# Attention tiles ordered long and short in turn, and the low part of k multiplied by the high part of q alone, the two maps in the two halves of the array's rows

## The chip, the cores and the metric

The kernel runs on one core of one Trainium2 chip. The metric is the device time of one execution in microseconds (us). Before the change the median of 3 runs is 2411.27 us (2409.47 to 2414.34).

## What is computed

The reference is one inference step of a two-layer encoder for a prompt (1 x 1024 tokens) and a sample group (8 streams x 16 tokens with 256 cached keys each), model width 1024, 8 heads. The part that the change touches is the differential attention: two softmax maps per head over 64-wide halves of q and k, chunk-causal for the prompt, unmasked over cache and new tokens for the sample.

```
def diff_attend(q, k, v, lam, mask):
    s = jnp.einsum('bqhmd,bkhmd->bhmqk', q, k).astype(jnp.float32) * (HEAD_DIM ** -0.5)
    if mask is not None:
        s = jnp.where(mask, s, -jnp.inf)
    p = jax.nn.softmax(s, axis=-1)
    a = p[:, :, 0] - lam * p[:, :, 1]
    return jnp.einsum('bhqk,bkhv->bqhv', a.astype(v.dtype), v)
```

Around it, each layer has an input projection, a pooling branch, gates (silu and sigmoid of projections), output projections and a LayerNorm.

## The kernel before, in words

Each layer runs in stages: projections of v, q and k, the pooling branch, then the attention stage (556 to 1010 us and 1750 to 2203 us of the profile), then the merge and the output projection. Large products are made in fp32r, with both operands split into a high and a low part: high x high, low x high, high x low.

The attention stage has two streams that one loop braids (lines 1384 to 1405). The filler (`filler`, line 968) computes gates for what follows: 16 weight tiles x 3 column groups x 8 steps, 384 steps of three matmuls with 384 columns (`tmm_steps`, lines 320 to 322), each chunk of 8 steps followed by a tanh on ScalarE (line 977) and, for 8 of the 16 weight tiles, a multiplication on VectorE (line 980). The attention (`attention`, line 1280) is a generator that yields a number after each piece of work; the loop multiplies it by `share` (line 1388) and runs so many filler steps. The numbers stand in `STEPS` (line 48): 54 a head.

A head has nine items: eight query tiles of 128 rows, 0 to 7, where tile i has 128 x (i + 1) keys, and the decode item "d" for all eight streams. An item's work is:

- `s1`: scores on TensorE into PSUM. A tile up to 3 uses one two-bank score buffer for both maps (lines 1062 to 1068), a longer tile one buffer for each map (lines 1079 to 1088); there are two buffers (`ps_two`). The operand `qs` holds q's high part in rows 0 to 63 and its low part in rows 64 to 127, and `kh` and `kl` hold k's high and low part twice, so one 128-row matmul gives (high + low of q) x (a part of k).
- `soft`: mask and negated maximum on VectorE (lines 1071 and 1072, or 1093 and 1094), exponentials with row sums on ScalarE (1076, 1096).
- `mix`: VectorE makes one map of two (1105 to 1109).
- `s2a`: transposes of the mixed map on TensorE (1119), copies by ScalarE to the tile `at` (1121). For "d" VectorE reduces the transposes into `azt` and `atl` (1196, 1198).
- `s2b`: the product with v on TensorE (1144; for "d" 1207 and 1214, on 32 columns of the array each), a copy to `osb` on VectorE (1126) and, later, squares on ScalarE.

An engine takes its instructions in the order in which this code issues them. In a slot (one item of the loop from line 1299 on) the order is: `s1` of item n, `s2a` of item n-2 (from slot 6 on, n-1), `soft` of n, first filler part, `s2b` of the same older item, `mix` of n, other work of the head, second filler part. The items come as "d", 0, 1, ... 7 (0, 1, "d", 2 to 7 in head 0), the last tile's second half in the next head's first slot.

For the next head, `prep_load` fetches q and k, `prep_split` splits them (ScalarE copies, lines 902 and 903, VectorE subtractions, 904 and 905), `load_dec`, `load_v` and `load_vc` fetch the decode keys and the values. All transfers are issued on SyncE's queue, in order. After a head, `post_a`, `post_f` and `post_b` normalise and transpose its output.

Of the kernel before, what the change touches and what calls it, by code (L numbers as in the profile page):

```python
# [17 lines left out]
P = 128  # L18
# [8 lines left out]
NG = 3  # L27
# [20 lines left out]
STEPS = [(3, 2), (2, 2), (4, 1), (2, 2), (2, 2), (3, 3, 4), (3, 4), (3, 4), (4, 4)]  # L48
MG = 4
HIP = False  # L50
HEAD0 = 8
YG = 2
# [11 lines left out]
def trunk(ctx, tc, a):  # L64
# [393 lines left out]
    for l in range(DEPTH):  # L458
# [435 lines left out]
        def prep_split(h, m):  # L894
# [6 lines left out]
            qs, kh, kl = mk("qs"), mk("kh"), mk("kl")  # L901
            S.copy(qs, sq)
            S.copy(kh, sk)
            V.tensor_tensor(out=qs[64:, :], in0=sq[64:, :], in1=qs[64:, :].bitcast(F32), op=ALU.subtract)
            V.tensor_tensor(out=kl, in0=sk, in1=kh.bitcast(F32), op=ALU.subtract)
            heads[h][m] = (qs, kh, kl)
# [47 lines left out]
        for tag, shape, bufs in (("osb", [P, 9, P], 2), ("gsb", [P, GW], 2), ("th", [P, GW], 3), ("atl", [P, P], 1),  # L954
                                 ("at", [P, 512], 2)):
            ap.tile(shape, F32, tag=tag, name=tag, bufs=bufs)
        for name in ("qs0", "kh0", "kl0"):
            ap.tile([P, SEQ], F32R, tag=name, name=name)
        ap.tile([P, 1024], F32, tag="p", name="p", bufs=3)
# [48 lines left out]
        ITEMS = ["d", 0, 1, 2, 3, 4, 5, 6, 7]  # L1008
# [45 lines left out]
        def s1_tile(h, i):  # L1054
# [7 lines left out]
            if n <= 512:  # L1062
                cw = max(n, 256)
                s = ps_two()
                for m in range(2):
                    qs, kh, kl = hd[m]
                    PE.matmul(s[:, m, :cw], qs[:, ql], kh[:, :cw], start=True, stop=False)
                    PE.matmul(s[:, m, :cw], qs[:, ql], kl[:, :cw], start=False, stop=True)
# [11 lines left out]
            sps = []  # L1080
            for m in range(2):
                qs, kh, kl = hd[m]
                s = ps_two()
                for b in range(2):
                    kc = slice(b * c, b * c + c)
                    PE.matmul(s[:, b, :c], qs[:, ql], kh[:, kc], start=True, stop=False)  # L1086
                    PE.matmul(s[:, b, :c], qs[:, ql], kl[:, kc], start=False, stop=True)  # L1087
                sps.append(s)
# [191 lines left out]
        def attention():  # L1280
# [9 lines left out]
            load_dec(0)  # L1290
# [4 lines left out]
            for h in range(H):  # L1295
                start_head(h)
                nxt = h + 1 < H
                items = ITEMS if h else [0, 1, "d"] + ITEMS[3:]
                for n, i in enumerate(items):
                    f1, f2 = STEPS[n][:2]  # L1300
                    soft = s1_dec(h) if i == "d" else s1_tile(h, i)
                    if n == 0:
# [423 lines left out]
```

## Time and profile before

| | |
|---|---|
| runs | 2411.27 us median (2409.47 to 2414.34, n = 3) |
| the profiled execution | 2411.42 us, its span 2409.6 us |
| granted TensorE clock, mean | 0.993 |
| busy share of the span | PE 96%, weight loads 90%, DVE 64%, ACT 41%, POOL 12% |
| DMA | 379.09 MB, 157 GB/s |
| attention stages | 556 to 1010 us, 1750 to 2203 us |

PE is TensorE's matmuls and PEld its weight loads, which overlap them; DVE is VectorE, ACT ScalarE, POOL GpSimd, SPq the queue of transfers. Lines such as L1144 are lines of the kernel. A timeline row gives the start in us, the duration, engine, line, operation, out<-in, shapes, count, and in brackets the idle time before it and what ended it. A row of waits gives the waiting instruction, what released it, and microseconds in total, the number of times, and where a third number stands the longest. A row of groups gives the count, then busy time in us and mean ns of one, then the idle time before. The duration of a matmul includes its way through the array; neighbours overlap, so the time that one occupies is read from the starts of two neighbours.

### The profile page before, as it was taken

How to read it: one execution, taken by the hardware profiler on the slowest of the kernel's cores; microseconds unless marked ns; L12 is line 12 of the kernel's file. 1: busy time of each engine (PE TensorE's matmuls, PEld its weight loads, DVE VectorE, ACT ScalarE, POOL GpSimd, SP SyncE). 2: the span in 40 equal slices, each digit the busy share in tenths (PEclk: the TensorE clock that was granted, in tenths of full speed). 3: DMA queues.
4: the chain of work that ended last, by engine and by line, in shares of the span. 5: the costliest groups of instructions: out<-in, count | busy, mean ns of one | idle time of the engine just before them, and what ended most of it. 6: DMA issues, size and time to landing. Idle time of an engine off the chain costs nothing.

```text
span 2409.6 us, 39819 instructions
## 1 busy us (share of the span) xinstructions
PE 2304.1 (96%) x14928; PEld 2157.8 (90%) x14928; DVE 1546.1 (64%) x2980; ACT 977.8 (41%) x2177; POOL 296.6 (12%) x312
## 2 busy tenths in 40 slices
PE   7999999998999999999999999999989999999998
PEld 6889999998888888898878999999988888889986
DVE  4477855546777777756524787546367777775855
ACT  8432234213555555523533232342145555554122
POOL 1023310000000000032100233000000000001433
PEclk9999999999999999999999999999999999999999
DMA  6643344656544554486336433445664555446942
GB/s 214 219 116 102 103 104 108 200 174 203 150 139 140 151 165 128 152 288 249 122 118 202 115 101 99 116 116 175 201 180 140 146 161 161 145 120 207 316 166 78
DMA packets 247714, 379.09 MB, mean 157 GB/s; under 512 B 49889, under 2 KB 190177, under 8 KB 247521
## 3 DMA queue, kind: packets, MB, share of 16 engines
q1 hardware_dynamic: 247520, 376.55, 50.9%
q8 instruction: 117, 1.92, 0.3%
q14 instruction: 77, 0.62, 0.1%
HBM read 259.67 MB, written 117.83 MB: 157 GB/s over the span
## 4 chain that ended last, share of the span: by engine, by line
PE 70%; DVE 11%; DMA 7%; ACT 6%; issue 4%; SPq 1%; POOL 1%; ACTq 0%; DVEq 0%; POOLq 0%
PE ps_lin L598 5%; PE ps_lin L596 5%; PE ps_lin L597 5%; PE ps_lin L320 5%; PE ps_lin L321 5%; PE ps_lin L322 5%; PE ps_tr L1144 4%; PE ps_tr L596 2%; PE ps_tr L598 2%; PE ps_tr L597 2%; PE ps_lin L335 2%; PE ps_lin L336 2%; PE ps_lin L334 2%; ACT p L1076 2%; PE ps_tr L1119 2%
## 5 line engine op out<-in xcount | busy, mean ns | idle before, releaser
L320 PE MATMUL ps_lin<-xh,wh 128*128 128x384 f32 x952 | 345.3, 363 | 1.1 <-ACT xh L1267 0.7
L322 PE MATMUL ps_lin<-xh,wl 128*128 128x384 f32 x952 | 321.3, 337 | 0.0
L321 PE MATMUL ps_lin<-xl,wh 128*128 128x384 f32 x952 | 320.7, 337 | 0.3 <-DVE xl L1270 0.2
L320 PEld LDWEIGHTS ps_lin<-xh,wh 128*128 128x128 f32 x952 | 180.4, 189 | 5.6 <-issue 2.8
L1144 PE MATMUL ps_tr<-vt,at 128*128 128x128 f32 x1152 | 156.2, 282 | 28.1 <-ACT at L1121 28.1
L1144 PEld LDWEIGHTS ps_tr<-vt,at 128*128 128x128 f32 x1152 | 147.2, 195 | 39.2 <-ACT at L1121 38.6
L321 PEld LDWEIGHTS ps_lin<-xl,wh 128*128 128x128 f32 x952 | 180.8, 190 | 1.1 <-DVE xl L1270 0.8
L322 PEld LDWEIGHTS ps_lin<-xh,wl 128*128 128x128 f32 x952 | 179.5, 189 | 0.0
L1121 ACT COPY at<-ps_tr 128x512 f32<-128x512 f32 (+1 forms) x192 | 85.8, 482 | 172.1 <-PE ps_tr L1119 172.1
L1096 ACT ACTIVATE p<-ps_two,anm 128x640 f32<-128x640 f32 (+3 forms) x128 | 122.3, 962 | 33.4 <-DVE anm L1094 29.8
L1076 ACT ACTIVATE p<-ps_two,anm 128x128 f32<-128x128 f32 (+3 forms) x128 | 66.4, 524 | 168.6 <-DVE anm L1072 160.3
L1094 DVE TENSOR_REDUCE anm<-ps_two 128x1 f32<-128x640 f32 (+3 forms) x128 | 131.2, 1025 | 4.4
L270 DVE TENSOR_TENSOR wl<-ws,wh 128x1024 fp32r<-128x1024 f32 (+1 forms) x74 | 86.0, 1162 | 70.8 <-ACT wh L265 67.6
L265 ACT CAST wh<-ws 128x1024 fp32r<-128x1024 f32 (+1 forms) x74 | 74.1, 1002 | 115.4 <-PE ps_lin L321 49.7
L640 POOL TENSOR_TENSOR tt<-tt 128x288 f32<-128x288 f32 x64 | 63.1, 986 | 420.4 <-DVE tt L639 257.2
L1108 DVE SCALAR_TENSOR_TENSOR p<-p,acc 128x128 f32<-128x128 f32 (+7 forms) x128 | 104.8, 818 | 4.5
L1086 PE MATMUL ps_two<-kh,qs 128*128 128x320 f32 (+3 forms) x256 | 91.0, 357 | 11.3 <-ACT p L1076 11.3
L1119 PE MATMUL ps_tr<-ident,p 128*128 128x128 f32 x576 | 84.4, 273 | 5.6 <-DVE r L1109 5.6
L1087 PE MATMUL ps_two<-kl,qs 128*128 128x320 f32 (+3 forms) x256 | 89.5, 352 | 0.0
L1126 DVE COPY osb<-ps_tr 128x128 f32<-128x128 f32 x144 | 41.3, 287 | 66.1 <-PE ps_tr L1144 60.4
L659 ACT COPY sb<-ps_lin 128x288 f32<-128x288 f32 x80 | 32.0, 400 | 123.3 <-PE ps_lin L598 118.8
L1119 PEld LDWEIGHTS ps_tr<-ident,p 128*128 128x128 f32 x576 | 69.2, 141 | 13.0 <-ACT xh L1267 6.2
(522 smaller groups left out, 6886.9 us busy)
## 6 DMA issues: line engine op xcount, KB each, us to landing
ws<-wt SPq DMA_DIRECT2D x96, 512.0 KB, 4.0
mt_d<-th SPq DMA_DIRECT2D x96, 192.0 KB, 3.2
fx<-q_d SPq DMA_DIRECT2D x128, 128.0 KB, 3.4
fx<-o_k SPq DMA_DIRECT2D x128, 128.0 KB, 3.3
st<-ck SPq DMA_DIRECT2D x32, 512.0 KB, 5.9
fx<-cv SPq DMA_DIRECT2D x32, 512.0 KB, 4.0
mt<-mt_d SPq DMA_DIRECT2D x42, 384.0 KB, 5.8
xT_d<-xs SPq DMA_DIRECT2D x36, 256.0 KB, 2.6
```

The lines of the kernel that those rows point to most:

```text
L320: PE.matmul(ps, wh[:, k, :], xh[:, k, :], start=(k == 0), stop=False),
L321: PE.matmul(ps, wh[:, k, :], xl[:, k, :], start=False, stop=False),
L322: PE.matmul(ps, wl[:, k, :], xh[:, k, :], start=False, stop=(k == nk - 1)))
L596: PE.matmul(ps, wh[:, k, :], oh[:, k, :], start=first and k == 0, stop=False, **more)
L597: PE.matmul(ps, wh[:, k, :], ol[:, k, :], start=False, stop=False, **more)
L598: PE.matmul(ps, wl[:, k, :], oh[:, k, :], start=False, stop=k == 3, **more)
L1076: S.activation(out=pt[m], in_=s[:, m, :n], func=AF.Exp, bias=nm[:, m:m + 1], accum_out=ls_[:, m:m + 1])
L1094: V.tensor_reduce(out=nm[:, m:m + 1], in_=s[:, :, :c], axis=AX.XY, op=ALU.max, negate=True)
L1096: S.activation(out=p[:, :n].rearrange("p (b c) -> p b c", b=2), in_=s[:, :, :c], func=AF.Exp, bias=nm[:, m:m + 1], accum_out=ls_[:, m:m + 1])
L1108: V.scalar_tensor_tensor(out=pt[0], in0=pt[1], scalar=cc, in1=pt[0], op0=ALU.mult, op1=ALU.add)
L1119: PE.transpose(tr[:, j * P:(j + 1) * P], p[:, (b0 + j) * P:(b0 + j + 1) * P], ident)
L1144: PE.matmul(o_ps, hd["at", i][b // 4][:, (b % 4) * P:(b % 4 + 1) * P], hd["vt", b // 4][:, b % 4, :], start=(b == 0), stop=(b == i))
```

## The change

Four things change, all in the attention stage.

**Items.** They come as 7, 3, 6, 2, 5, 1, 4, 0, "d" (in the last head 7, 3, 6, 2, 5, "d", 4, 1, 0), in one flow of 72 slots over all heads, with two more slots at the end. In slot j: `s1` of item j, `s2a` of item j-2, `soft` of j, `mix` of j-1, squares, first filler part, `s2b` of j-2, other work, second filler part. The loads, splits and post-processing move to other slots: the split of the next head's second map to the start of slot 8, the decode keys to slot 2 of their own head, the decode values to slot 8 (in the last head slot 3).

**Filler.** `STEPS` has 52 steps a head, and `share` is computed for 28 steps fewer (`REST`), so that 365 of the 384 steps fall into the attention generator and the others run after it.

**Low part of k.** The product of q's low part with k's low part is left out. The low parts of k of both maps share one tile `kl`: map 0 in rows 0 to 63, map 1 in rows 64 to 127. For map 1, `qs` has its high part in rows 64 to 127. The high matmuls of both maps come first, on 128 rows; then the low matmuls on 64 rows each, map 0 in the upper half of the array's rows and map 1 in the lower half, in turn.

**Small.** The tiles that were allocated ahead at the start of the stage no longer are, and what the last heads' output waits for before its split is 5 rounds in place of 2 (line 1382).

```diff
-STEPS = [(3, 2), (2, 2), (4, 1), (2, 2), (2, 2), (3, 3, 4), (3, 4), (3, 4), (4, 4)]
+STEPS = [(2, 3), (5, 1), (3, 2), (3, 4), (3, 2), (3, 4), (3, 2), (3, 3), (3, 3)]
+REST = 28
...
-            qs, kh, kl = mk("qs"), mk("kh"), mk("kl")
+            qs, kh = mk("qs"), mk("kh")
+            if m == 0:
+                heads[h]["kl"] = mk("kl")
+            kl = heads[h]["kl"]
+            hi, lo = (slice(m * 64, m * 64 + 64), slice(64 - m * 64, 128 - m * 64))
             S.copy(qs, sq)
             S.copy(kh, sk)
-            V.tensor_tensor(out=qs[64:, :], in0=sq[64:, :], in1=qs[64:, :].bitcast(F32), op=ALU.subtract)
-            V.tensor_tensor(out=kl, in0=sk, in1=kh.bitcast(F32), op=ALU.subtract)
-            heads[h][m] = (qs, kh, kl)
+            V.tensor_tensor(out=qs[lo, :], in0=sq[lo, :], in1=qs[lo, :].bitcast(F32), op=ALU.subtract)
+            V.tensor_tensor(out=kl[hi, :], in0=sk[hi, :], in1=kh[hi, :].bitcast(F32), op=ALU.subtract)
+            heads[h][m] = (qs, kh, kl[hi, :], hi)
...
-        ITEMS = ["d", 0, 1, 2, 3, 4, 5, 6, 7]
+        ITEMS = [7, 3, 6, 2, 5, 1, 4, 0, "d"]
+        LAST = [7, 3, 6, 2, 5, "d", 4, 1, 0]
...
                 for m in range(2):
-                    qs, kh, kl = hd[m]
+                    qs, kh, _, _ = hd[m]
                     PE.matmul(s[:, m, :cw], qs[:, ql], kh[:, :cw], start=True, stop=False)
-                    PE.matmul(s[:, m, :cw], qs[:, ql], kl[:, :cw], start=False, stop=True)
+                for m in range(2):
+                    qs, _, kl, hi = hd[m]
+                    PE.matmul(s[:, m, :cw], qs[hi, ql], kl[:, :cw], start=False, stop=True)
...
-            sps = []
+            sps = [ps_two() for _ in range(2)]
             for m in range(2):
-                qs, kh, kl = hd[m]
-                s = ps_two()
                 for b in range(2):
-                    kc = slice(b * c, b * c + c)
-                    PE.matmul(s[:, b, :c], qs[:, ql], kh[:, kc], start=True, stop=False)
-                    PE.matmul(s[:, b, :c], qs[:, ql], kl[:, kc], start=False, stop=True)
-                sps.append(s)
+                    PE.matmul(sps[m][:, b, :c], hd[m][0][:, ql], hd[m][1][:, b * c:b * c + c], start=True, stop=False)
+            for b in range(2):
+                for m in range(2):
+                    qs, _, kl, hi = hd[m]
+                    PE.matmul(sps[m][:, b, :c], qs[hi, ql], kl[:, b * c:b * c + c], start=False, stop=True)
...
+            flow = [(h, n, i) for h in range(H) for n, i in enumerate(ITEMS if h < H - 1 else LAST)]
+            for j in range(len(flow) + 2):
+                h, n, i = flow[j] if j < len(flow) else (H, j - len(flow), None)
+                back = flow[j - 2] if j >= 2 else None
+                last = h == H - 1
+                f1, f2 = STEPS[n]
+                if n == 0 and h < H:
+                    start_head(h)
+                if n == 8 and not last:
+                    if h + 1 < H:
+                        prep_split(h + 1, 1)
+                soft = None
+                if i is not None:
                     soft = s1_dec(h) if i == "d" else s1_tile(h, i)
+                if back:
+                    s2a(back[0], back[2])
+                if soft:
                     soft()
+                if 0 < j <= len(flow):
+                    mix(flow[j - 1][0], flow[j - 1][2])
+                do_squares()
+                yield f1
+                if back:
+                    s2b(back[0], back[2])
...
+                yield f2
...
-                ylive.append([h, g, 2])
+                ylive.append([h, g, 5])
...
-        share = len(gate_order) * NG * KD / (H * sum(map(sum, STEPS)) + HEAD0)
+        share = (len(gate_order) * NG * KD - REST) / (H * sum(map(sum, STEPS)) + HEAD0)
```

What stands on TensorE for tile 5 of the second head before: the eight score matmuls, map 0 in buffer `ps_two_6730` and map 1 in `ps_two_6735`, each high matmul followed by its low one, and the transposes of tile 4.

```order
L1086 MATMUL ps_two_6730<-kh_6047,qs_6046 128x384
L1087 MATMUL ps_two_6730<-kl_6048,qs_6046 128x384
L1086 MATMUL ps_two_6730<-kh_6047,qs_6046 128x384
L1087 MATMUL ps_two_6730<-kl_6048,qs_6046 128x384
L1086 MATMUL ps_two_6735<-kh_6283,qs_6282 128x384
L1087 MATMUL ps_two_6735<-kl_6284,qs_6282 128x384
L1086 MATMUL ps_two_6735<-kh_6283,qs_6282 128x384
L1087 MATMUL ps_two_6735<-kl_6284,qs_6282 128x384
L1119 MATMUL ps_tr_6740<-ident_72,p_6635 128x128 x4
```

The same place on TensorE now, for tile 6 of the first head, with the transposes of tile 7 behind it (L1085 and L1089 are the high and the low matmul, L1120 the transposes).

```order
L1085 MATMUL ps_two_5757<-kh_5524,qs_5523 128x448 x2
L1085 MATMUL ps_two_5758<-kh_5657,qs_5656 128x448 x2
L1089 MATMUL ps_two_5757<-kl_5525,qs_5523 128x448
L1089 MATMUL ps_two_5758<-kl_5525,qs_5656 128x448
L1089 MATMUL ps_two_5757<-kl_5525,qs_5523 128x448
L1089 MATMUL ps_two_5758<-kl_5525,qs_5656 128x448
L1120 MATMUL ps_tr_5767<-ident_72,p_5699 128x128 x4
```

The low matmuls have moved behind all the high ones and alternate between the two maps, and both read one tile `kl_5525`; both buffers are complete only with the last two rows.

On VectorE, the decode item and tile 0 of the second head before: maximum of "d" (L1166), its mixing (L1179 to L1182), then maximum of tile 0 (L1072) and its mixing (L1105 to L1109).

```order
L1166 TENSOR_REDUCE dnm_6337<-ps_two_6311 128x2
L980 SCALAR_TENSOR_TENSOR th_6351<-th_6351,ps_lin_6257 128x384
L1126 COPY osb_5703<-ps_tr_6356 128x128
L1179 RECIPROCAL drc_6366<-dls_6339 128x2
L1180 TENSOR_SCALAR drc_6366<-drc_6366,sgn_4682 128x2
L1182 TENSOR_SCALAR p_6340<-p_6340,drc_6366 128x384 x2
L1071 MEMSET ps_two_6381 64x2x64
L1072 TENSOR_REDUCE anm_6380<-ps_two_6381 128x2
L1105 RECIPROCAL ar2_6399<-als_6379 128x1
L1107 SCALAR_TENSOR_TENSOR acc_6401<-als_6379,nlam_4681,ar2_6399 128x1
L1108 SCALAR_TENSOR_TENSOR p_6388<-p_6388,acc_6401 128x128
```

And on VectorE now, tiles 4 and 1 of the second head: both maps' maximum of tile 4 (L1095), then the mixing of tile 1, whose probabilities are `p_6608` and whose sums are `als_6593`.

```order
L1094 MEMSET ps_two_6674 64x64
L1095 TENSOR_REDUCE anm_6673<-ps_two_6674 128x1
L1094 MEMSET ps_two_6675 64x64
L1095 TENSOR_REDUCE anm_6673<-ps_two_6675 128x1
L1106 RECIPROCAL ar2_6704<-als_6593 128x1
L1108 SCALAR_TENSOR_TENSOR acc_6706<-als_6593,nlam_4681,ar2_6704 128x1
L1109 SCALAR_TENSOR_TENSOR p_6608<-p_6608,acc_6706 128x256
L1110 RECIPROCAL r1_6234<-als_6593 128x1
L979 SCALAR_TENSOR_TENSOR th_6715<-th_6715,ps_lin_6587 128x384
```

An item's mixing has moved from behind its own maximum to behind the maximum of the item after it.

More of the change, by code (lines that the diff above doesn't have):

```diff
@@ L952, in trunk @@
         ap = ap_ctx.enter_context(tc.tile_pool(name=f"a2_{l}", bufs=1, reuse_waits="tile"))
[L954 to L959, printed above, removed]
         cmask = ap.tile([P, 2, P], F32, name="cmask")
@@ L1288, in mix @@
                 mix_dec(h) if i == "d" else mix_tile(h, i)
-            load_dec(0)
             load_v(0, 0)
@@ L1357, in attention @@
-            s2a(H - 1, 7)
-            yield 3
-            s2b(H - 1, 7)
+            flow = [(h, n, i) for h in range(H) for n, i in enumerate(ITEMS if h < H - 1 else LAST)]
[11 more added lines that the diff above has]
+                if i is not None:
+                    soft = s1_dec(h) if i == "d" else s1_tile(h, i)
+                if back:
+                    s2a(back[0], back[2])
+                if soft:
+                    soft()
+                if 0 < j <= len(flow):
[4 more added lines that the diff above has]
+                    s2b(back[0], back[2])
+                if h > 0 and n == 0 and h < H:
+                    load_v(h, 1)
+                if 0 < h < H:
+                    if n == 2:
+                        post_a(h - 1)
+                        g_load(h - 1, 0)
+                        g_load(h - 1, 1)
+                    if n == 3:
+                        post_f(h - 1)
+                    if 5 <= n <= 7:
+                        post_b(h - 1, n - 5)
+                    if n == 5:
+                        g_load(h - 1, 2)
+                    if n == 7:
+                        posted.append(h - 1)
+                if h < H:
+                    if n == 2:
+                        load_dec(h)
+                        if h + 1 < H:
+                            prep_load(h + 1, 0)
+                    if n == 3 and last:
+                        load_vc(h)
+                    if n == (4 if last else 6):
+                        mk_qz(h)
+                if h + 1 < H:
+                    if n == 5:
+                        prep_split(h + 1, 0)
+                        prep_load(h + 1, 1)
+                        load_v(h + 1, 0)
+                    if n == 8:
+                        load_vc(h)
+                yield f2
```

58 lines of the change are left out of this document (removed).

## The prediction

> **What bounds the kernel now.** I read the page first, then the busy time by stretches of the attention stage, then the list of waits, then the timeline of single items.
>
> ```profile
> span 2409.6 us, 39819 instructions
> PE 2304.1 (96%) x14928; PEld 2157.8 (90%) x14928; DVE 1546.1 (64%) x2980; ACT 977.8 (41%) x2177; POOL 296.6 (12%) x312
> ```
>
> TensorE is the bound: 96% busy, and the next engine has 64%. What can be won by order is therefore the time in which it stands still. The profiled execution took 2411.42 us, 1.8 us more than its span, and the runs shown have a median of 2411.27, so what I take from the span I take from either. The stretches of both layers' attention stages (start, the seven heads from the second part of head 0 on, end; columns: start:end, length, busy time of PE, PEld, DVE, ACT and POOL with instructions in brackets, granted clock, DMA share, GB/s):
>
> ```profile
> 556.00:590.00 34.00, 29.85 (x208) 26.48 (x206) 21.66 (x57) 13.01 (x36) 0.00 (x0) 0.95 0.64 195
> 590.00:965.00 375.00, 352.81 (x2555) 327.85 (x2556) 281.51 (x680) 202.45 (x535) 14.62 (x20) 1.00 0.49 147
> 996.00:1010.00 14.00, 10.51 (x52) 9.71 (x51) 8.15 (x16) 7.53 (x15) 2.00 (x2) 0.76 0.74 233
> 1750.00:1785.00 35.00, 28.45 (x209) 24.98 (x207) 22.89 (x61) 14.23 (x41) 0.00 (x0) 1.00 0.66 204
> 1785.00:2160.00 375.00, 354.19 (x2555) 329.25 (x2556) 280.94 (x677) 201.12 (x531) 14.62 (x20) 1.00 0.50 146
> 2191.00:2203.00 12.00, 8.93 (x51) 8.13 (x50) 7.28 (x15) 5.92 (x13) 1.83 (x2) 0.86 0.84 262
> ```
>
> TensorE idles 22.2 and 20.8 us in the steady parts (375 less 352.81 and 354.19), 4.2 and 6.6 at the starts, 3.5 and 3.1 at the ends, 60 us in all. At the ends the granted clock falls as well (0.76 and 0.86), which costs up to 14 x 0.24 = 3.4 and 12 x 0.14 = 1.7 us more. Who it waits for, over the whole program; the weight load in front of the matmul is what stands in the queue, so I take its waits:
>
> ```profile
> PEld ps_tr L1144 <- ACT at L1121: 38.6, 32, 2.3
> PEld ps_two L1086 <- ACT p L1076: 15.3, 16, 1.3
> PEld ps_tr L1207 <- issue: 7.0, 13, 1.4
> PE ps_two L1157 <- DMA vt<-o_v: 5.2, 2, 2.6
> ```
>
> The first is the value product waiting for the transposed probabilities. One such wait in order of time:
>
> ```profile
> 635.18 0.96 DVE L1072 TENSOR_REDUCE anm<-ps_two 128x2 f32<-128x768 f32 x1
> 636.17 0.58 ACT L1076 ACTIVATE p<-ps_two,anm 128x384 f32<-128x384 f32 x1 [3.41 <-DVE anm L1072]
> 636.74 0.57 ACT L1076 ACTIVATE p<-ps_two,anm 128x384 f32<-128x384 f32 x1
> 637.44 0.17 DVE L1105 RECIPROCAL ar<-als 128x1 f32<-128x1 f32 x1 [1.10 <-ACT p L1076]
> 637.59 0.37 ACT L1121 COPY at<-ps_tr 128x256 f32<-128x256 f32 x1
> 638.01 0.71 PE L1144 MATMUL ps_tr<-vt,at 128*128 128x128 f32 x4 [1.55 <-ACT at L1121]
> ```
>
> ScalarE had nothing to do for 3.41 us, because VectorE reached the maximum late; then two exponentials stood ahead of the copy that TensorE needed. VectorE for its part sat 1.10 us until the exponentials ended, since before the change the mixing of an item follows its own maximum. The two engines take turns, and TensorE pays.
>
> **The change: order.** Afterwards VectorE takes the maximum of item j and only then mixes item j-1, whose exponentials are a slot old, and the transposes and products of j-2 come a slot later still. Nothing in such a slot waits for what the same slot has begun. I price the first two kinds of wait (38.6 + 15.3 = 53.9 us) at a third of what they were: 36 us gone. The load of the decode product (L1207) gets a first part of 5 steps in place of 4; I take 4 of its 7.0 us. What is late next is the item after a long one. A long item takes both score buffers, and now both maps end together, so the next item's scores wait for maximum and exponential of the first map:
>
> ```profile
> L1094 DVE TENSOR_REDUCE anm<-ps_two 128x1 f32<-128x1024 f32 x2 | 2.4, 1224 | 0.1
> L904 DVE TENSOR_TENSOR qs<-fx,qs 64x1024 fp32r<-64x1024 f32 x2 | 2.4, 1222 | 0.1
> L905 DVE TENSOR_TENSOR kl<-fx,kh 128x1024 fp32r<-128x1024 f32 x2 | 2.5, 1226 | 0.1
> L1096 ACT ACTIVATE p<-ps_two,anm 128x1024 f32<-128x1024 f32 x2 | 2.2, 1124 | 0.0
> ```
>
> ```profile
> 671.27 0.33 PE L321 MATMUL ps_lin<-xl,wh 128*128 128x384 f32 x1
> 671.45 0.34 PE L322 MATMUL ps_lin<-xh,wl 128*128 128x384 f32 x1
> ```
>
> For tile 7 that is 1.22 + 1.12 = 2.3 us and the hand-overs. Behind it stand 5 filler steps x 0.84 of three matmuls each, and a matmul takes 0.175 (671.27 to 671.45): 2.2 us, so it is short by the hand-overs and by whatever VectorE is late. The split of the next head's second map now stands ahead of the decode item's maximum in VectorE's queue, with two subtractions of 1.22 us, and its result is due one item later, where it was due two later. And VectorE is well filled; this stretch is about one head:
>
> ```profile
> 695.00:750.00 55.00, 51.68 (x374) 47.95 (x374) 42.70 (x103) 29.73 (x78) 2.10 (x3) 1.00 0.52 153
> ```
>
> It has 42.7 us of work in a head that I expect to last about 52 (375/7 = 53.6, less 2 by order, less 1.2 of filler steps moved behind the last head, and 1 more by the halves, below), so it will sometimes be late. I put 0.6 us a head on these three, 16 heads, 10 us. Order in the steady heads: 36 + 4 - 10 = 30 us less, between 0 (VectorE's queue passes every wait on) and 43 (all the idle time gone). That kl is now written on 64 rows gains nothing: 64 rows take 1222 ns (L904), 128 take 1226 (L905). The queue of transfers has a wait of its own, in the first layer's stage:
>
> ```profile
> SPq L1044 <- DVE qs L904: 76.1, 7, 15.3
> ```
>
> The decode values wait there 11 us a head for a subtraction, with weight loads behind them. Now the split is issued ahead of the item and the values are asked for after its first part, so the wait shrinks; they are due two items on, and I cost this at nothing. If they came late, the wait would show on the decode product, up to some 2 us a head. The decode keys are asked for six items before use, some 34 us.
>
> **The start and the end.** At the start the first decode item goes from third to last place, and its 2.6 us wait in each layer (5.2 in the list) goes with it; the splits of head 0 are waited for as before. 5 us less, between 2 and 9. The end:
>
> ```profile
> 996.28 0.34 PE L322 MATMUL ps_lin<-xh,wl 128*128 128x384 f32 x1
> 999.43 1.06 PE L1119 MATMUL ps_tr<-ident,p 128*128 128x128 f32 x8 [2.82 <-DVE r L1109]
> 1001.88 3.78 PE L1144 MATMUL ps_tr<-vt,at 128*128 128x128 f32 x16 [0.68 <-ACT at L1121]
> ```
>
> Tile 7 was last, with nothing behind it; 16 products took 3.78 us at a lowered clock. Afterwards tiles 1 and 0 are last, and 11 filler steps x 0.84 stand over their chains, with 19 of the 384 steps left over for what follows the last head (8 x 52 + 8 + 11 = 435 units x 0.8396 give 365). These steps are moved, not removed: no gain of their own. Of 6.6 us idle and 5.1 of clock I take 9.5 as gone, between 4 and 11.7.
>
> **The change: the halves of the rows.** What the low part takes now, by the starts of neighbours of one width:
>
> ```profile
> 558.90 0.28 PE L1067 MATMUL ps_two<-kh,qs 128*128 128x256 f32 x1
> 559.02 0.28 PE L1068 MATMUL ps_two<-kl,qs 128*128 128x256 f32 x1
> 990.48 0.39 PE L1086 MATMUL ps_two<-kh,qs 128*128 128x512 f32 x1
> 990.71 0.39 PE L1087 MATMUL ps_two<-kl,qs 128*128 128x512 f32 x1
> ```
>
> 0.12 us at 256 columns and 0.23 at 512; in between I take 0.15, 0.17, 0.21. A head's low part of one map is 0.12 + 0.12 + 0.17 + 0.23 for tiles 0 to 3 and 2 x (0.15 + 0.17 + 0.21 + 0.23) for 4 to 7: 2.16 us. If the two maps run side by side, 2.16 us a head is saved, 34.5 us in 16. No 64-row matmul is in the trace. The nearest rows are the decode matmuls on 32 columns of the array, going in and out:
>
> ```profile
> L1214 PE MATMUL ps_tr<-fx,azt 128*32 128x128 f32 x512 | 19.4, 273 | 0.0
> ...
> 629.79 1.14 PE L1214 MATMUL ps_tr<-fx,azt 128*32 128x128 f32 x30
> 630.86 0.45 PE L320 MATMUL ps_lin<-xh,wh 128*128 128x384 f32 x1
> 631.14 0.34 PE L321 MATMUL ps_lin<-xl,wh 128*128 128x384 f32 x1
> ...
> 671.71 0.64 PE L1157 MATMUL ps_two<-st,qz 128*32 128x256 f32 x8
> 675.52 1.95 PE L1144 MATMUL ps_tr<-vt,at 128*128 128x128 f32 x16
> 677.22 0.42 PE L320 MATMUL ps_lin<-xh,wh 128*128 128x384 f32 x1
> ```
>
> Going in, 0.26 us pass from 671.45 to 671.71 in place of 0.175: 0.09 lost. Going out, the last L1214 began at about 630.66 (the group's end less the 0.27 that one lasts), so L320 came 0.20 later; a 128-column pass takes 0.11 (16 from 675.52 to 677.22), so 0.09 is lost again. L320's successor came after 0.28 in place of 0.175: its weights were loaded in the open, 0.11. A 128-column load in the open on the way in costs the same 0.11. One visit to the halves: 0.09 + 0.11 + 0.09 + 0.11 = 0.40 us. Eight items a head make 128 visits, 51 us. Against the 34.5 saved this is 17 us more (51.2 less 34.5). Its ends: 34.5 less (no price for the visit) and 51 more (a visit's price and nothing side by side). I take the 17, because the decode rows show both things in one place: eight passes of 256 columns are over 0.64 us after the first began, so narrow ones do run together, and the switch costs. The Trainium skill, TensorEngine Tiling (Array Packing), Key Properties, says that changing the tiling mode drains TensorE and that tiles work independently. By it both halves of my price hold, and this is the rule that speaks against the change; the column rows agree, and no run here shows it for rows.
>
> **The sum.** 2411.4 - 30 - 5 - 9.5 + 17 = 2384 us.
>
> **The rivals.** (1) The halves cost nothing to enter: 2384 - 51 = 2333; VectorE's 42.7 us a head would then stand against some 49 of span, and give some of it back, to about 2350. The same page, Overview, gives up to twice the speed for a contraction of at most 64, and by that alone one would expect this. Against it stand the decode rows. (2) Slower: the halves are entered at the full price but the two maps run one after the other. Then 51 in place of 17: 2384 + 34 = 2418. It decides itself where the second of a pair starts 0.1 us or more after the first; the trace has side-by-side work for columns alone, not for rows. (3) The order gains nothing in the steady heads, since VectorE at 42.7 us a head hands each delay on: 2384 + 30 = 2414. For it speaks how close VectorE is, against it its idle time for exponentials. (4) Neither price nor pairing, the halves change nothing: 2384 - 17 = 2367.
>
> **The numbers.** Chances: the forecast 0.50 (alone 2370 to 2401, from the bounds of start, end and half the order term), (1) 0.17, (2) 0.13, (3) 0.12, (4) 0.08. A difference of 0.2% (4.8 us) is about what a measurement of this kernel can tell from none. Faster by more, under 2406.6: 0.49 of the forecast, 0.17, 0.02 of (3), 0.08: 0.76. Within: 0.01 of the forecast, 0.04 of (2), 0.07 of (3): 0.12. Slower, over 2416.2: 0.09 of (2) and 0.03 of (3): 0.12. The range from 2342 to 2418 leaves out the fast part of (1), 0.10, and the slow half of (2), 0.07.
>
> **What would show it.** Right: L1145 waits for copies about a third as long as L1144 did; VectorE's reciprocals no longer wait for exponentials; no fall of the clock at the ends of the stages; two low-part matmuls begin within 0.01 us of each other, and the row after them begins 0.2 us late. Wrong: the gap around a low pair is missing (rival 1), the second of a pair starts 0.1 us after the first (2), or the steady stretches keep their 20 us of idle time with VectorE over 85% busy (3).

## The result, and the profile after

The changed kernel takes 2370.98 us (median of 4 runs, 2367.71 to 2373.66) against 2410.75 (2409.47 to 2414.34, 4 runs) before: a ratio of 0.9832, 95% interval 0.9815 to 0.9849. That is 39.8 us less. The prediction had 2384, 27 less, and a range from 2342 to 2418.

The page of the changed kernel, as far as it answers to the rows of before:

```profile
span 2370.6 us, 39878 instructions
PE 2304.5 (97%) x14928; PEld 2110.6 (89%) x14928; DVE 1538.8 (65%) x2980; ACT 981.3 (41%) x2177; POOL 301.1 (13%) x312
```

TensorE has as much busy time as before (2304.1 then); the span has shrunk around it. The steady parts of the two layers, in stretches of 355 us:

```profile
590.00:945.00 355.00, 348.18 (x2532) 302.37 (x2532) 282.75 (x686) 204.30 (x534) 17.80 (x20) 1.00 0.54 158
1766.00:2121.00 355.00, 348.18 (x2532) 302.38 (x2531) 282.92 (x687) 204.24 (x533) 17.78 (x20) 1.00 0.53 158
```

TensorE idles 6.8 us in each, where it idled 22.2 and 20.8 in 375. For the whole attention stage I cut both kernels at the same two places, the first score matmul and the first matmul of the product behind the attention. Before:

```profile
558.90:1005.30 446.40, 416.05 (x2974) 385.70 (x2974) 330.13 (x789) 238.73 (x626) 14.62 (x20) 0.99 0.50 150
1752.90:2199.50 446.60, 415.66 (x2975) 385.23 (x2974) 330.01 (x789) 238.46 (x626) 14.62 (x20) 0.99 0.51 150
```

And after:

```profile
558.50:980.90 422.40, 414.30 (x2975) 362.03 (x2974) 327.00 (x792) 238.24 (x625) 20.40 (x25) 1.00 0.53 156
1733.50:2156.80 423.30, 414.54 (x2975) 362.14 (x2974) 327.98 (x793) 238.33 (x625) 20.38 (x25) 1.00 0.52 156
```

The stage is 24.0 and 23.3 us shorter, 47.3 in all. Its idle time (the length less TensorE's busy time) went from 61.3 us (30.35 + 30.94) to 16.9 (8.1 + 8.76). The span is only 39.0 shorter, so 8 us came back elsewhere; that is followed up below. Who TensorE waits for now, in its list of weight loads:

```profile
PEld ps_tr L1120 <- issue: 18.9, 74, 0.4
PEld ps_two L1089 <- issue: 17.7, 64, 0.4
...
PEld ps_two L1070 <- issue: 9.8, 32, 0.4
PEld ps_two L1067 <- ACT p L1097: 7.8, 18, 0.6
PEld ps_two L1085 <- ACT p L1078: 7.3, 11, 1.3
...
PEld ps_tr L1145 <- ACT at L1122: 2.0, 8, 0.3
PEld ps_two L321 <- ACT xh L1268: 2.0, 4, 0.8
```

The value product's wait for its copies, 38.6 us before, is 2.0. The wait for a score buffer was 15.3 and is 7.3 + 7.8 = 15.1, at two lines. New are three waits for "issue" (L1120, L1089, L1070), which are no waits for another engine: they stand where the low matmuls begin and end.

VectorE's own list shows the other half. Before, its reciprocals, with which an item's mixing begins, waited for ScalarE's exponentials:

```profile
DVE ar L1105 <- ACT p L1076: 54.9, 56, 1.3
```

After the change no such row is left in the list. One item with its neighbours in order of time:

```profile
688.20 0.69 DVE L1074 TENSOR_REDUCE anm<-ps_two 128x2 f32<-128x512 f32 x1
688.39 0.48 ACT L1122 COPY at<-ps_tr 128x384 f32<-128x384 f32 x1 [2.04 <-PE ps_tr L1120]
688.80 0.15 DVE L1106 RECIPROCAL ar<-als 128x1 f32<-128x1 f32 x1
688.92 0.48 ACT L1078 ACTIVATE p<-ps_two,anm 128x256 f32<-128x256 f32 x1
689.25 1.02 DVE L1109 SCALAR_TENSOR_TENSOR p<-p,acc 128x768 f32<-128x768 f32 x1
```

VectorE takes the maximum of tile 1, then mixes tile 5 (768 wide), the item before it, with no wait in front of the reciprocal, while ScalarE copies the transposes of tile 2, one item older still, ahead of the new exponentials. In the picture of before, the copy stood behind two exponentials and the reciprocal waited 1.10 us.

### The profile page after: what moved, and what is told of

Its sections match the earlier page's. It is cut to its first block, busy times and chain, and to the rows that moved or that the text cites. A ratio compares the mean times of both kernels' runs of the same rounds, so it can differ in the third digit from the quotient of the medians.

```text
span 2370.6 us, 39878 instructions
## 1 busy us (share of the span) xinstructions
PE 2304.5 (97%) x14928; PEld 2110.6 (89%) x14928; DVE 1538.8 (65%) x2980; ACT 981.3 (41%) x2177; POOL 301.1 (13%) x312
## 4 chain that ended last, share of the span: by engine, by line
PE 81%; DVE 6%; DMA 5%; ACT 3%; issue 3%; SPq 1%; POOL 1%; DVEq 0%; ACTq 0%; POOLq 0%
PE ps_lin L321 6%; PE ps_lin L322 6%; PE ps_lin L323 6%; PE ps_tr L1145 5%; PE ps_lin L599 5%; PE ps_lin L597 5%; PE ps_lin L598 5%; PE ps_tr L1120 3%; PE ps_lin L336 3%; PE ps_lin L337 2%; PE ps_lin L335 2%; PE ps_tr L597 2%; PE ps_tr L599 2%; PE ps_tr L598 2%; PE ps_two L1085 2%
## 5 line engine op out<-in xcount | busy, mean ns | idle before, releaser
L1122 ACT COPY at<-ps_tr 128x512 f32<-128x512 f32 (+2 forms) x192 | 86.6, 482 | 208.8 <-PE ps_tr L1120 208.7
L1097 ACT ACTIVATE p<-ps_two,anm 128x1024 f32<-128x1024 f32 (+3 forms) x128 | 122.3, 962 | 33.7 <-DVE anm L1095 23.1
L1095 DVE TENSOR_REDUCE anm<-ps_two 128x1 f32<-128x1024 f32 (+3 forms) x128 | 131.1, 1024 | 4.4
L641 POOL TENSOR_TENSOR tt<-tt 128x288 f32<-128x288 f32 x64 | 62.9, 982 | 419.4 <-DVE tt L640 257.1
L1109 DVE SCALAR_TENSOR_TENSOR p<-p,acc 128x1024 f32<-128x1024 f32 (+7 forms) x128 | 104.8, 818 | 4.5
L1120 PE MATMUL ps_tr<-ident,p 128*128 128x128 f32 x576 | 91.1, 284 | 5.5 <-ACT at L1122 4.1
L1078 ACT ACTIVATE p<-ps_two,anm 128x512 f32<-128x512 f32 (+3 forms) x128 | 66.4, 524 | 71.5 <-DVE ar L1106 59.2
L1120 PEld LDWEIGHTS ps_tr<-ident,p 128*128 128x128 f32 x576 | 62.5, 141 | 31.1 <-issue 18.9
L1513 POOL TENSOR_TENSOR mg<-mt 128x384 f32<-128x384 f32 x42 | 59.1, 1411 | 118.3 <-DVE mt L1512 112.1
L642 POOL TENSOR_TENSOR tt<-tt 128x288 f32<-128x288 f32 x64 | 73.2, 1143 | 0.0
L1085 PE MATMUL ps_two<-kh,qs 128*128 128x512 f32 (+3 forms) x256 | 61.9, 357 | 4.9 <-ACT p L1078 4.2
```

What stands on the lines that cost most here:

```text
L1085: PE.matmul(sps[m][:, b, :c], hd[m][0][:, ql], hd[m][1][:, b * c:b * c + c], start=True, stop=False)
L1095: V.tensor_reduce(out=nm[:, m:m + 1], in_=s[:, :, :c], axis=AX.XY, op=ALU.max, negate=True)
L1097: S.activation(out=p[:, :n].rearrange("p (b c) -> p b c", b=2), in_=s[:, :, :c], func=AF.Exp, bias=nm[:, m:m + 1], accum_out=ls_[:, m:m + 1])
L1109: V.scalar_tensor_tensor(out=pt[0], in0=pt[1], scalar=cc, in1=pt[0], op0=ALU.mult, op1=ALU.add)
L1120: PE.transpose(tr[:, j * P:(j + 1) * P], p[:, (b0 + j) * P:(b0 + j + 1) * P], ident)
```

## The experiments

Unless another number is given, differences are against the medians of the changed kernel (2371.0) or of the order alone (2351.3). The kernel before, run beside each experiment, took 2410.9 to 2411.8; ratios are against it. The edits are shown in part, against the changed kernel if nothing else is said; `...` marks what is left out.

### The order alone

The order of after with the low part as before: both parts of q times the low part of k, on 128 rows, each low matmul behind its high one. The items, loads, filler numbers and small changes stay.

```diff
...
-                for m in range(2):
-                    qs, _, kl, hi = hd[m]
-                    PE.matmul(s[:, m, :cw], qs[hi, ql], kl[:, :cw], start=False, stop=True)
+                    PE.matmul(s[:, m, :cw], qs[:, ql], kl[:, :cw], start=False, stop=True)
...
+                    PE.matmul(s[:, b, :c], qs[:, ql], kh[:, kc], start=True, stop=False)
+                    PE.matmul(s[:, b, :c], qs[:, ql], kl[:, kc], start=False, stop=True)
...
```

> The changed kernel with the low part as it was before: both parts of q times the low part of k on 128 rows, kl twice for each map, each map's buffer complete in turn. Only the order, the loads and the filler numbers of the change remain. Theory A (a visit to the halves of the array's rows costs more than the pairing saves; the changed kernel's trace has 0.09 + 0.11 on the way in and 0.09 + 0.05 on the way out, 128 x 0.34 = 44 us, against 34.5 saved): about 9 us faster than the changed kernel's 2371, 2358 to 2366. Theory B (the pairing is worth having): slower than 2371, up to 2371 + 34 = 2405 if the visits hide in waits.

Measured: 2351.33 us (2346.98 to 2353.67), ratio 0.9746 [0.9733, 0.9758]. The order by itself takes 60 us off, and the halves of the rows put 19.7 back, about twice the 9 of theory A; what the other half is, the run with both buffers completed together shows below. The stages of this kernel:

```profile
559.70:971.70 412.00, 406.32 (x2974) 381.67 (x2974) 326.26 (x791) 238.30 (x624) 20.28 (x25) 1.00 0.54 159
1724.00:2137.00 413.00, 406.63 (x2975) 381.70 (x2974) 327.12 (x792) 238.47 (x624) 20.31 (x25) 1.00 0.53 159
```

They idle 5.7 and 6.4 us, and TensorE is busy in them for 812.95 us, where it was for 831.71 before the change.

### The halves alone

The kernel before, with the low part as in the changed kernel. The edit is against the kernel before; the splits and the long tiles, left out here, change as in the change itself.

```diff
...
-                    PE.matmul(s[:, m, :cw], qs[:, ql], kl[:, :cw], start=False, stop=True)
+                for m in range(2):
+                    qs, _, kl, hi = hd[m]
+                    PE.matmul(s[:, m, :cw], qs[hi, ql], kl[:, :cw], start=False, stop=True)
...
```

> The kernel before, with only the halves of the rows: its own order of items, fillers and loads. Theory A: slower than before by what the visits cost beyond the pairing, less what falls into times when TensorE waits anyway: +3 to +17 us, 2414 to 2428. Theory B: faster by up to 34 us, 2376 or more.

Measured: 2410.01 us (2404.74 to 2415.56, 12 runs), ratio 0.9994 [0.9985, 1.0003]. No difference: neither a cost nor a gain of the sizes expected. The waits of TensorE in this kernel (L1149 is the value product, L1089 a long tile's high matmul, L1093 and L1074 are the low matmuls, L1124 the transposes):

```profile
PEld ps_tr L1149 <- ACT at L1126: 27.1, 29, 2.0
PEld ps_tr L1124 <- issue: 21.0, 83, 0.4
PEld ps_two L1089 <- ACT p L1082: 19.9, 16, 1.6
PEld ps_two L1093 <- issue: 17.8, 64, 0.4
...
PEld ps_two L1074 <- issue: 9.9, 32, 0.4
```

The price of the visits is there, at the same three places as in the changed kernel and of nearly the same size (21.0 + 17.8 + 9.9 against 18.9 + 17.7 + 9.8). In return the wait for copies has shrunk from 38.6 to 27.1: TensorE comes later to a place where it would have stood anyway. The wait for score buffers has grown, from 15.3 to 19.9, so these rows alone do not show that the sum comes out at nothing; the time does. The same edit is free in a kernel that waits and costs 19.7 us in one that does not.

### Twice as many visits

The changed kernel, with the high and low matmuls of each half of a long tile's keys taken together, so that tiles 4 to 7 enter the halves twice: 64 visits more.

```diff
-            for m in range(2):
-                for b in range(2):
+            for b in range(2):
+                for m in range(2):
                     PE.matmul(sps[m][:, b, :c], hd[m][0][:, ql], hd[m][1][:, b * c:b * c + c], start=True, stop=False)
-            for b in range(2):
                 for m in range(2):
                     qs, _, kl, hi = hd[m]
```

> The changed kernel with two visits to the halves for each long tile in place of one: high matmuls of the first bank, their low pair, high of the second bank, their low pair. 4 tiles x 16 heads = 64 visits more, each 0.09 + 0.11 in and 0.09 + 0.11 out (the next is an fp32r matmul) = 0.40 us. Theory A: +25 us, about 2396. If a visit costs nothing that counts (rival): 2371, within 3 us.

Measured: 2400.56 us (2399.32 to 2401.27), ratio 0.9951 [0.9938, 0.9964]: 29.6 us more for 64 visits, 0.46 us each. The first row of its list of waits has doubled, from 64 to 128 times:

```profile
PEld ps_two L1088 <- issue: 33.8, 128, 0.4
```

So a visit has a price, and it is a price by the visit, not by the column: the columns are the same. Tile 4 in order of time, with its first visit, the high matmuls of the second half of the keys, and its second visit:

```profile
700.70 0.42 PE L1088 MATMUL ps_two<-kl,qs 64*128 64x320 f32 x2
701.04 0.56 PE L1085 MATMUL ps_two<-kh,qs 128*128 128x320 f32 x2
701.53 0.42 PE L1088 MATMUL ps_two<-kl,qs 64*128 64x320 f32 x2
```

### The mixing back in its own slot

The changed kernel, with an item's mixing after the first filler part of its own slot, where it stood before the change; the transposes still come two slots later.

```diff
-                if 0 < j <= len(flow):
-                    mix(flow[j - 1][0], flow[j - 1][2])
                 do_squares()
...
+                if j < len(flow):
+                    mix(h, i)
```

> The changed kernel with the mixing of an item back in the item's own slot, after the first filler part, as it was before; the order of the items and the two slots of lag stay. Theory C (VectorE no longer waiting for the exponentials of its own slot is what took the waits away): the value product waits for copies again, +15 to +30 us, 2386 to 2401. Rival D (short items between the long ones and two slots of lag are enough, whatever VectorE's order): within 5 us of 2371.

Measured: 2417.61 us (2413.76 to 2423.6), ratio 1.0026 [1.0016, 1.0035]: 46.6 us more, beyond what was expected. With this one step undone the whole gain is gone. VectorE waits for the exponentials again:

```profile
DVE ar L1106 <- ACT p L1078: 31.9, 40, 1.6
```

The waits of TensorE:

```profile
PEld ps_two L1085 <- ACT p L1078: 23.7, 20, 3.0
...
PEld ps_two L1067 <- ACT p L1097: 12.6, 22, 1.2
```

And two items in order of time:

```profile
686.03 0.57 ACT L1078 ACTIVATE p<-ps_two,anm 128x384 f32<-128x384 f32 x1
686.72 0.16 DVE L1106 RECIPROCAL ar<-als 128x1 f32<-128x1 f32 x1 [1.10 <-ACT p L1078]
...
689.74 0.96 DVE L1095 TENSOR_REDUCE anm<-ps_two 128x1 f32<-128x768 f32 x1
```

The 1.10 us of VectorE's wait for the exponentials are back, to the hundredth. The mixing and what stands behind it then push the next maximum (689.74), and TensorE waits for score buffers. It does not wait for copies, as theory C expected: the value product's wait stays at 2.6 us. So the place of the mixing is not what took the wait for copies away. The two rows are 36.3 us where the changed kernel had 15.1, 21 of the 46.6; the stages idle 44.1 us in place of 16.9, and the rest is busy time, in part at a lowered clock (0.98 granted in the second layer's stage, 1.00 in the changed kernel's).

### Both buffers complete together

The order alone, on 128 rows, but with the long tiles' low matmuls placed as in the changed kernel: all high ones first, then the low ones in turn between the maps. Of the halves only the place is left.

```diff
...
                 for m in range(2):
-                    qs, _, kl, hi = hd[m]
-                    PE.matmul(sps[m][:, b, :c], qs[hi, ql], kl[:, b * c:b * c + c], start=False, stop=True)
+                    qs, _, kl = hd[m]
+                    PE.matmul(sps[m][:, b, :c], qs[:, ql], kl[:, b * c:b * c + c], start=False, stop=True)
```

> The order alone (2351) with the long tiles' low matmuls on 128 rows, but placed as in the changed kernel: all high ones first, then the low ones of both maps in turn, so that both score buffers are complete only at the end. No visit to halves of the rows. Theory E (of the 20 us by which the halves made the order worse, about 9 are the visits by their rows, and the rest is that the first map's maximum starts later): 8 to 12 us slower than the order alone, 2359 to 2363. Rival F (the visits alone cost it): within 3 us of 2351.

Measured: 2363.03 us (2360.68 to 2366.48), ratio 0.9802 [0.9787, 0.9816]: 11.7 more than the order alone. The waits for score buffers in this kernel:

```profile
PEld ps_two L1063 <- ACT p L1091: 7.6, 18, 0.8
...
PEld ps_two L1079 <- ACT p L1072: 6.8, 6, 1.5
```

And in the order alone, where the first map's buffer is complete after the fourth of the eight score matmuls and not after the seventh:

```profile
PEld ps_two L1082 <- ACT p L1072: 3.1, 6, 1.0
...
PEld ps_two L1063 <- ACT p L1092: 1.0, 2, 0.5
```

14.4 against 4.1 us, which is 10.3 of the 11.7. So more than half of what the halves cost is not the array at all: the maximum of the first map starts later, because its low matmuls stand behind the high ones of the second.

### No low part at all

The changed kernel with all low-part matmuls left out; its scores lack the term of k's low part.

```diff
...
-                    PE.matmul(s[:, m, :cw], qs[hi, ql], kl[:, :cw], start=False, stop=True)
...
-                    PE.matmul(sps[m][:, b, :c], qs[hi, ql], kl[:, b * c:b * c + c], start=False, stop=True)
...
```

> The changed kernel without any matmul of the low part of k: that part of the scores is left out, the splits are still made. Theory G (TensorE is what bounds the stage): the time goes by all that the low part takes there, 128 x 0.34 us of visits and 34.5 us of pairs, 78 us, and the earlier maximum: 2283 to 2303. Rival H (VectorE, 40 us of work in a head of 51, takes over as the bound): at most half of it, 2330 or more.

Measured: 2309.55 us (2306.82 to 2310.93), ratio 0.958 [0.9564, 0.9596]: 61.4 us less than the changed kernel. That lies between the two theories, nearer to G. By rows the low part should take 34.5 us of columns (two maps side by side) and 128 x 0.35 = 45 of visits (below), 79, and the 11.7 of the late buffer on top; so 61.4 of some 90 came out as time. The kernel is then still mostly bound by TensorE. Of the rest, 13.5 us went into waits: the stages idle 30.4 us (391.3 and 392.6 less 376.63 and 376.87), where the changed kernel's idle 16.9. The remainder is not accounted for.

### No filler steps kept for the end

The changed kernel with all 384 filler steps spread over the heads.

```diff
-REST = 28
+REST = 0
```

> The changed kernel with REST = 0: all filler steps run inside the attention generator, none behind the last head. The prediction's end term (9.5 us) partly rests on the 19 moved steps: if they are what covers the last chains, +4 to +10 us, 2375 to 2381, with the clock down at the ends of the stages. If the short last items do it alone: within 3 us of 2371.

Measured: 2384.27 us (2379.85 to 2388.01), ratio 0.9888 [0.9872, 0.9904]: 13.3 more than the changed kernel, and more than the 4 to 10 expected. The two stages are 3.5 us longer (424.2 and 425.0 us), the stretches behind them 8.9 (110.5 and 116.0 us where the changed kernel takes 106.1 and 111.5). The waits between 940 and 1015 us of this kernel:

```profile
PEld ps_tr L1145 <- ACT at L1122: 3.9, 2, 2.1
PEld ps_two L322 <- DVE xl L1271: 3.8, 6, 1.2
PEld ps_lin L322 <- DVE xl L1271: 1.7, 3, 0.8
```

The value product of the last items and the splits behind the attention stand in the open. The last items are short in this kernel too; it is the 19 steps behind them that cover the end, and most of what they cover lies behind the attention.

### The order alone, with two variations

First with the wait of 2 rounds (as before) in place of 5 before the last heads' output is split, then with 44 steps kept for the end in place of 28.

```diff
-                ylive.append([h, g, 5])
+                ylive.append([h, g, 2])
```

> The order alone (2351) with the small change undone: 2 rounds in place of 5 between the load of the last stage's operand and its split. In the order alone the stretch behind the attention is 4 us longer than before in each layer, with short waits for these splits. If the 5 rounds make them: 3 to 8 us faster, 2343 to 2348. If the loads themselves come late: within 3 us of 2351.

Measured: 2348.39 us (2347.25 to 2350.88), ratio 0.9741 [0.9727, 0.9756].

```diff
-REST = 28
+REST = 44
```

> The order alone (low part on 128 rows) with 44 steps left out of the share in place of 28, so that some 14 more of the 384 filler steps follow the last head. Leaving none over cost the change 13 us. Theory K: 19 steps of 0.525 us already outlast the end chains, so more of them change nothing there, and the heads have less cover: 0 to 5 us more than the order alone (2351). Rival L: the chains behind the last head still want cover: 3 to 8 us less.

Measured: 2349.18 us (2347.56 to 2351.12), ratio 0.9742 [0.9728, 0.9757]. Neither can be told from the order alone (0.9746 [0.9733, 0.9758]), and neither decides between its two expectations: 2.9 us less with 2 rounds, 2.2 less with 44 steps. The traces say where time moved. From the end of the attention stage to the same later place the first layer takes 106.8 us in the order alone, 105.6 with 2 rounds, and 102.8 with 44 steps. So the 5 rounds are not the main reason why this stretch is long; more steps behind the last head cover it, but the heads miss them: with 44 steps the stage takes 414.1 us in place of 412.0.

### Long and short in turn, or in ascending order

For these two the tile of the probabilities has four buffers in place of three, since an ascending order holds more of them at a time. The first is the control.

```diff
-                    p = ap.tile([P, 1024], F32, tag="p", name="p", bufs=3)
+                    p = ap.tile([P, 1024], F32, tag="p", name="p", bufs=4)
```

> The changed kernel with four buffers for the probabilities in place of three; a control for the next run, nothing else changed. A tile's probabilities live for three slots in the new flow (exponentials in j, mixing in j+1, transposes in j+2), and VectorE's and TensorE's lists of waits after the change show no wait for one of these buffers, so theory I and its rival both expect within 4 us of the change (2367 to 2375).

Measured: 2368.55 us (2367.59 to 2373.77), ratio 0.9829 [0.9813, 0.9846], not told from the changed kernel. The second has the same four buffers and this edit:

```diff
-        ITEMS = [7, 3, 6, 2, 5, 1, 4, 0, "d"]
-        LAST = [7, 3, 6, 2, 5, "d", 4, 1, 0]
+        ITEMS = [0, 1, 2, 3, 4, 5, 6, 7, "d"]
+        LAST = [0, 1, 2, 3, 4, "d", 5, 6, 7]
```

> As the run before (four buffers of probabilities), with the items as 0, 1, ... 7, d in every head (0, 1, 2, 3, 4, d, 5, 6, 7 in the last), in the new flow. Theory I: the turn of long and short counts by itself, because a long item takes both score buffers and the next long one can begin only when the maximum and the exponential of both maps are through; four long items in a row in each head, three hand-overs of 0.5 to 0.6 us more, 24 to 30 us over the run before, and a wait of the high matmuls for the exponentials of 20 us or more in TensorE's list. Rival J: what gains is the mixing one item later and the transposes two items later, the filler steps stand between any two items anyway: within 6 us in the steady heads, and 5 to 8 more at the end of each layer, where tile 7 is last again: 5 to 20 us in all.

Measured: 2370.32 us (2369.5 to 2371.4), ratio 0.983 [0.9816, 0.9844]: 1.8 from the control, not told apart. Theory I falls, which was mine. Long tiles one after another do wait for their buffers, but hardly more in all:

```profile
PEld ps_two L1085 <- ACT p L1097: 16.4, 24, 1.8
...
PEld ps_two L1085 <- ACT p L1078: 2.3, 2, 1.1
```

These are 18.7 us, where the control has 14.8 (7.8 at L1067 and 7.0 at L1085): after a long item the next one waits for the first map's buffer, whether it is long or short. Rival J comes nearer, but its time, 5 to 20 us, was too high as well: the 5 to 8 us for a long tile at the end did not come either. That the steps kept for the end cover it is likely, but no run shows it. So the steps of the new order whose undoing costs time are the mixing one item later and the filler kept for the end. The turn of long and short, after which the change is named, gains nothing that these runs can show.

## Why the prediction came out as it did

**The mechanism of the order: right.** An item's mixing behind the next item's maximum takes VectorE out of ScalarE's way: its waits for exponentials are gone from the list (54.9 us at one row before). The mixing put back costs 46.6 us and brings the same 1.10 us wait. So the gain needs this step. That it is enough isn't shown: no run moves the mixing alone in the kernel before.

**Its size: the term that was too small.** All terms of the order come to 44.5 us in the prediction (30 + 5 + 9.5), with 10 already off for late score buffers; the order alone measured 60. Three things stand behind the difference:

- I priced the wait for copies at a third of 38.6 us. It went to 2.0, a twentieth. What took it away is open. Half of it before (16 of the 32 waits, 18.3 us) stood at tile 1, whose transposes came two items later already, as in the new order, so the lag alone isn't the reason. Nor is it the place of the mixing (2.6 us with the mixing put back) or the turn of long and short (1.5 in ascending order).
- The 10 us for new waits were put into the order, but 11.7 us come with the place of the low matmuls (both buffers complete together), and such waits are 4.1 us in the order alone. The prediction named the cause and booked it in the wrong term.
- I took idle time for all the time that TensorE stands. In the order alone the stage has 49.2 us less idle time (61.3 to 12.1), but is 68 us shorter (893.0 to 825.0): 18.8 us were busy time. The two traces show where it went, if the distance from each matmul's start to the next one's is set against the usual one of its shape (0.175 us at 384 columns). 6.6 us are matmuls at half the granted clock, for which I had counted 5.1 at the ends; there are two such stretches more, at 570.6 and 1785.7 us, of 3.4 us each (granted clock 0.50 and 0.51). 8.1 us are the last matmuls before a stop of TensorE, which are counted as busy for some 0.17 us in which nothing new starts, and 3.9 us the first matmuls after a stop, which hold it longer than usual. The two stages have 68 stops before and 21 in the order alone.

**Given back behind the attention: not priced.** The prediction ended with the stage. Behind it, to the same place in both kernels, this stretch took 102.9 us before and 106.2 after:

```profile
1005.30:1108.20 102.90, 102.55 (x588) 101.90 (x588) 64.47 (x77) 29.05 (x38) 31.02 (x24) 0.99 0.81 280
```

```profile
980.90:1087.10 106.20, 104.42 (x587) 102.08 (x587) 62.51 (x72) 31.23 (x40) 28.91 (x21) 0.98 0.82 276
```

The loss in order of time:

```profile
993.67 0.44 PE L322 MATMUL ps_two<-xl,wh 128*128 128x384 f32 x1 [0.15 <-DVE xl L1271]
...
994.75 0.44 PE L321 MATMUL ps_two<-xh,wh 128*128 128x384 f32 x1 [0.45 <-ACT xh L1268]
995.34 0.44 PE L322 MATMUL ps_two<-xl,wh 128*128 128x384 f32 x1 [0.15 <-DVE xl L1271]
...
996.41 0.60 PE L321 MATMUL ps_lin<-xh,wh 128*128 128x384 f32 x1 [0.46 <-ACT xh L1268]
...
998.45 0.52 PE L323 MATMUL ps_tr<-xh,wl 128*128 128x384 f32 x1
998.77 0.52 PE L321 MATMUL ps_tr<-xh,wh 128*128 128x384 f32 x1
```

The last heads' output is split later, relative to the product that needs it. There are four short waits (0.15, 0.45, 0.15 and 0.46 us), and then the clock falls: it is 0.76 between 993 and 1000 us, and matmuls start 0.32 us apart (998.45 to 998.77) in place of 0.175. The same stretch of the second layer went from 107.8 to 111.5 us, so 7.0 of the 8 us are found. Why the split is late is not settled: the run with 2 rounds has most of the loss too, and 44 steps kept for the end take it away but give about half of it back in the stage. "No fall of the clock at the ends of the stages" was thus right for the stage (1.00 in its last 12 us, in both layers) and wrong behind it.

**The smaller terms** came about as priced. The decode product's load waits 4.0 us where it waited 7.0; the 5.2 us at the first decode item are gone; and the queue's wait ahead of the decode values, costed at nothing, fell from 151.9 to 9.5 us over the program.

**The halves of the rows: right in total, wrong in what it is made of.** 17 us were forecast and 19.7 measured (2371.0 less 2351.3). Tile 4 in the changed kernel shows a visit; up to 693.00 us the window holds the first two low matmuls:

```profile
692.75 0.31 PE L1085 MATMUL ps_two<-kh,qs 128*128 128x320 f32 x1
692.99 0.42 PE L1089 MATMUL ps_two<-kl,qs 64*128 64x320 f32 x2
```

And the whole visit:

```profile
692.32 0.74 PE L1085 MATMUL ps_two<-kh,qs 128*128 128x320 f32 x4
692.99 0.56 PE L1089 MATMUL ps_two<-kl,qs 64*128 64x320 f32 x4
693.48 0.87 PE L1120 MATMUL ps_tr<-ident,p 128*128 128x128 f32 x6
```

- Two low matmuls begin within 0.01 us of each other: the pairs run side by side, and rival 2 is out. The Trainium skill, TensorE: Matmul & The Clock Gate, Part 3 on row and column tiling, gives about 4 ns between the starts of such neighbours. The trace agrees: 124 of the 128 pairs on tiles 4 to 7 begin within 5 ns.
- Going in takes 0.24 us (692.75 to 692.99), where the high matmuls follow each other in 0.145 (three steps from 692.32 to 692.75 are 0.43): 0.095 lost, where 0.09 was forecast.
- Two pairs take 0.29 us of columns side by side, and 0.49 pass until the next row: 0.20 lost inside and going out, as forecast (0.09 + 0.11).
- The last 0.11 of the 0.40 was for the weight load in the open after the visit. What follows is a transpose, not a filler matmul, and the next row starts 0.164 us after it where the others are 0.109 apart: 0.055. A visit is 0.35 by these rows, 128 of them 45 us, less 34.5 saved is 10.
- The other 11.7 us are the late first buffer. 10 and 11.7 together are 21.7, against 19.7.

So the forecast of 17 came close with a visit that was somewhat too dear and without the second part, which stood in the order's term; that the two errors nearly cancel is luck. The doubled visits cost 0.46 us each, more than these rows give. The first of a tile's two visits ends before a 128-row score matmul, and there the rows (701.04 to 701.53) have 0.49 us for two high matmuls and the way in, which should be 0.29 + 0.095: 0.105 lost after the visit in place of 0.055, so 0.40 a visit. The last 0.06 us I can't place. The rule that spoke against the change (the Trainium skill, TensorEngine Tiling (Array Packing), Key Properties: a change of mode drains TensorE) agrees with the rows for the halves, 0.095 us lost going in and 0.20 inside and going out.

**The rivals.** The halves are not free to enter and not without pairing (rivals 1 and 4): both rows are in the trace. By the time alone rival 4 (2367) would fit better than the forecast (2384); the order alone, at 2351.3, shows that the halves do cost something. Rival 3, by which VectorE would hand every delay on, fell: TensorE idles 6.8 us in 355 while VectorE is busy for 282.75, 80%. The mixing in its own slot shows how near it was: the same work in VectorE's queue, one slot earlier, costs all of the gain.

**The best version** with the whole low part of k is the order without the halves, 2351.3 us (0.9746) or one of its two variations, which can't be told from it. In the kernel before, the low part on 64 rows looked free because TensorE waited anyway.

## What to carry to other kernels

When one engine waits for another inside an item, put the wait's far end behind the next item's work and not behind its own; count the gain from the whole wait, and look for what is given back behind the stage. A part of a change that costs nothing by itself can still cost once another part has removed the waits that hid it, so run each part alone and together. Before packing matmuls into halves of the array, weigh the saved columns against a price for each visit, and check whether the new order of matmuls completes a buffer later that another engine starts on.

## What was not expected of the hardware

Entering and leaving the 64-row halves costs about as much as the 32-column tiles of the decode items do: 0.095 us in and 0.20 inside and going out, 0.35 to 0.46 us a visit in all, while neighbours in the two halves begin within 0.01 us. At 320 columns a pair of low matmuls saves 0.145 us, so a visit with two pairs (0.29 saved) does not pay for itself. At 512 columns (0.23 each by the rows of before) two pairs save 0.46, as much as the dearest of these prices; no run has the long tiles alone in the halves.
